# S5 output operators built by VectorE, and all of layer 1's S5 operators built in the buffer of layer 0's states

## The chip, the cores and the metric

The kernel runs on one core of a Trainium2 chip. Its engines are TensorE (PE in the profile; its weight loads are PEld), VectorE (DVE), ScalarE (ACT), GpSimd (POOL) and SyncE (SP), which here issues every DMA from one queue, in order. Each engine works through its own instructions in order and waits on semaphores for the others. The metric is the device time of one execution in microseconds; smaller is better.

## What is computed

The reference is a two-layer backbone over 256 context and 512 latent tokens of width 1024. Each layer normalizes and modulates the tokens, projects them once, sends parts of the result through three scans (Mamba-2 SSD, gated linear attention GLA, and S5), joins them, projects back and adds the residual. The S5 part is what the change touches. Its operators depend on parameters alone, not on the tokens:

```
lam_bar = jnp.exp(lam * jnp.exp(log_step[d].astype(f32))[:, None])
b_bar = ((lam_bar - 1.0) / lam)[..., None] * bmat
cmat = lax.complex(c_re[d].astype(f32), c_im[d].astype(f32))

def scan_fn(u, h0):
    bu = jnp.einsum("blgh,gph->blgp", u.astype(jnp.complex64), b_bar)
    h = s5_scan(bu, h0, lam_bar)
    return jnp.einsum("blgp,ghp->blgh", h, cmat).real, h[:, -1]
...
y_c, y_l = bidirectional(make_scan(0), make_scan(1), ctx_args, lat_args, h0)
```

There are 32 groups of 16 channels, each with 64 complex states, in two directions and two layers.

## The kernel before

The 768 tokens of a channel are cut into 96 blocks of 8 steps. For one layer the S5 part runs in these steps:

- `s5_lambda(l)` computes the powers 0 to 8 of `lam_bar` (tile `s5p`, 128 x 576; the eighth also in tile `l8`) by some 90 small DVE instructions on 128 x 32, transposes by PE, and a matrix for the input side that goes to DRAM (`lpD`).
- `s5_in_map(l, bi)`, eight times, loads a block of B (`in_s5b`) and a block of `lpD`, multiplies them on DVE (L360 to L363) and leaves an operator `bl` of 128 x 1024.
- the channels `u` come from four projection tiles and are regrouped through DRAM; PE multiplies them by `bl` (L608), and ACT, L612 and L613 fill the recurrence's input `st` (tile `xy`).
- the recurrence over 96 blocks is the loop at L643 to L646: four DVE instructions a step, 25 steps a layer, with scratch `hn` in buffer `bA`; then ACT and DVE copy the states into `hn`.
- `s5_out_map(l, bi)`, sixteen times, builds in a buffer `cs` the output operators: one POOL instruction on 128 x 32 (L375) and six on 128 x 288 (L380 to L385), two stores to `clD`, eight PE products (L394), two copies by ACT, two small DVE instructions (L400, L401) and two stores to `gD`.
- the output `y5` is three PE products a group (L687 to L689), from `gD`, `clD` and `hn`.

The other parts named below: the projections (PE L492 and L494, whose weights are loaded into `wr`, copied by ACT into `wh`, and whose rest `wl` is formed at L416 on POOL or, every third time, on DVE); the gates (L511); GLA (PE L732 for its gates, DVE L738 to L799); the convolution in front of SSD (DVE L856 to L865); the SSD scan, whose first instruction on DVE is the mask at L910.

In layer 0 the kernel before builds, ahead of its own projections, the operators of layer 1 too: `s5_lambda(1)` and the eight `s5_in_map(1)` work in one half of `bA`. What they make goes to DRAM: the powers to `pwD`, the input operators to `blD`. The sixteen `s5_out_map(1)` come after `y5`. Layer 1 loads the input operators two at a time, inside the loop that fills `st`.

Buffers carry a tag and a count: `bA` and `bB` have one each, `cs` three, `s5p` and `l8` one each, `wr` two. A tile that takes a tag waits until the earlier holder is done with it, in the order of the program. Within that a scheduler sets each engine's order from its own estimate of the times.

Of the kernel before, what the change touches and what calls it, by code (L numbers as in the profile page):

```python
# [41 lines left out]
def hybrid_backbone_kernel(  # L42
# [146 lines left out]
    pwD = dram([128, 704], "pwD1")  # L189
# [47 lines left out]
    pw0, l8_0 = T("s5p", [128, 576], 1), T("l8", [128, 128], 1)  # L237
# [126 lines left out]

    def s5_out_map(l, bi, pw, buf):

        gs = 2 * bi
        w5, tmp, cb, cn = cuts(buf, 576, 288, 128, 32)
        gt = tmp[:, 0:240]
        dma(cb, s5cb[l, bi])  # L370
        b0 = cb[:, 64:128].rearrange("p (a x) -> p a x", a=2)

        w54 = w5.rearrange("p (a g k h) -> p a g k h", a=2, g=2, k=9)
        t54 = tmp.rearrange("p (g k h) -> p g k h", g=2, k=9)
        G.tensor_scalar(cn, cb[:, 0:32], -1.0, None, MUL)  # L375
        shp = [128, 2, 9, 16]
        pr, pi = (pw[:, :, a, gs : gs + 2].rearrange("p k g -> p g k").unsqueeze(3).to_broadcast(shp) for a in range(2))
        cr, ci, cm = (x.rearrange("p (g h) -> p g h", g=2).unsqueeze(2).to_broadcast(shp)
                      for x in (cb[:, 0:32], cb[:, 32:64], cn))
        G.tensor_tensor(w54[:, 0], pr, cr, MUL)  # L380
        G.tensor_tensor(t54, pi, ci, MUL)
        G.tensor_tensor(w54[:, 0], w54[:, 0], t54, SUB)  # L382
        G.tensor_tensor(w54[:, 1], pi, cm, MUL)
        G.tensor_tensor(t54, pr, ci, MUL)
        G.tensor_tensor(w54[:, 1], w54[:, 1], t54, SUB)  # L385
        for d in range(2):
            h = slice(64 * d, 64 * d + 64)
# [88 lines left out]
    def layer(l, u):  # L476
# [117 lines left out]
        if not last:  # L594
            for bi in range(16):
                s5_out_map(0, bi, pw_(pw0), cs())
        st = T("xy", [128, 8, NT], 1).rearrange("p a t -> p (a t)").rearrange("p (i r g) -> p i r g", i=96, r=2)
        for bi in range(16):
            if bi % 2 == 0:
                blt = bls[bi // 2] if not last else wa[:, 4096 + 1024 * (bi // 2 % 2) : 5120 + 1024 * (bi // 2 % 2)]  # L600
                if last:
                    dma(blt, blD[bi // 2])
            bl = blt.rearrange("p (a g x) -> p a g x", a=2, g=4)[:, :, 2 * (bi % 2) : 2 * (bi % 2) + 2, :]
# [494 lines left out]
        for m in range(8):  # L1098
# [32 lines left out]
    s5_lambda(0, cs(), cs(), cs(512), cs(), cs(), pw0, l8_0)  # L1131
# [18 lines left out]
    t = [bct(), bct()]  # L1150
    wa0, wb0 = big("bA"), big("bB")
    bls = [wb0[:, 1024 * i : 1024 * i + 1024] for i in range(6)] + [wa0[:, 4096 + 1024 * i : 5120 + 1024 * i] for i in range(2)]
    lps, bbs = [a[:, 0:1024] for a in t], [a[:, 1024:1536] for a in t]
    for bi in range(8):
        s5_in_map(0, bi, lps[bi % 2], bbs[bi % 2], wa0[:, 3360:3872], bls[bi])
# [9 lines left out]
    u = norm_in(1, hx, nrm)  # L1165
    hx, acc = layer(1, u)
# [93 lines left out]
```

## Time and profile before

| | |
|---|---|
| median of three runs | 1703.96 us (1702.16 to 1710.37) |
| profiled execution | 1712.97 us, span 1711.3 us |
| PE busy | 1418.1 us (83%) |
| DVE busy | 1168.2 us (68%) |
| POOL busy | 783.2 us (46%) |
| ACT busy | 679.9 us (40%) |
| mean granted TensorE clock | 0.901 |

Busy shares are means over the whole span. The rows further down cut it into stretches, since another engine sets the pace in each. Layer 0 ends near 1050 us. The profiled execution is 9 us longer than the median of the runs.

### The profile page before, as it was taken

The page shows a single profiled execution, that of the slowest core. Times are in us where ns is not written, and L with a number is a line of the kernel's source. Part 1 is how long each engine was busy: PE and PEld are TensorE (multiplying, and loading weights), DVE is VectorE, ACT ScalarE, POOL GpSimd, SP SyncE. Part 2 cuts the span into 40 slices and gives each one's busy share as a digit, 9 for nine tenths or more (in the row PEclk, how much of TensorE's full clock was granted, in tenths as well). Part 3 has the DMA queues.
Part 4 walks back from the last instruction along what each step waited for, and adds up shares of the span by engine and source line. Part 5 has one row for each costly group of instructions (what it writes and reads, how often), then busy time and mean ns, then how long its engine had stood idle before and what let it go on. Part 6 is the DMA issues. An engine that isn't in the chain of part 4 may idle for free.

```text
span 1711.3 us, 23539 instructions
## 1 busy us (share of the span) xinstructions
PE 1418.1 (83%) x8536; PEld 1145.2 (67%) x8536; DVE 1168.2 (68%) x1992; ACT 679.9 (40%) x1220; POOL 783.2 (46%) x716
## 2 busy tenths in 40 slices
PE   3867766888989779977779999997889989967886
PEld 2656655777966557755668786886678777745665
DVE  7977558995477567679994127289835986688752
ACT  4312223225342336646553124343345345545442
POOL 3615647632268843445463141164123323656454
PEclk9788987898988889988889999998988999988998
DMA  8474654332543354444455745522363242344542
GB/s 308 124 185 135 178 150 135 93 118 71 176 123 86 100 165 140 142 154 139 128 187 188 282 135 178 189 85 80 111 193 107 64 139 93 119 138 145 184 131 96
DMA packets 139885, 243.55 MB, mean 142 GB/s; under 512 B 31992, under 2 KB 72568, under 8 KB 139768
## 3 DMA queue, kind: packets, MB, share of 16 engines
q1 hardware_dynamic: 139768, 242.04, 45.3%
q8 instruction: 67, 1.10, 0.3%
q14 instruction: 50, 0.41, 0.1%
HBM read 192.81 MB, written 49.18 MB: 141 GB/s over the span
## 4 chain that ended last, share of the span: by engine, by line
PE 25%; DVE 18%; DMA 13%; POOL 6%; issue 4%; ACT 4%; SPq 0%; DVEq 0%; ACTq 0%; POOLq 0%
PE pl L492 7%; PE pl L1062 6%; DMA bA<-acsD 5%; DMA bB<-acsD 3%; PE pc L494 2%; PE pc L1064 2%; DVE xy L863 1%; DMA wr<-in_wblk 1%; ACT bA L121 1%; POOL wl L416 1%; DVE bB L916 1%; DVE bA L916 1%; DVE xy L645 1%; DMA cs<-zD 1%; DVE bA L644 1%
## 5 line engine op out<-in xcount | busy, mean ns | idle before, releaser
L492 PE MATMUL pl<-hl,wh 128*128 128x512 f32 (+1 forms) x1184 | 411.5, 414 | 15.9 <-DVE ev L511 12.3
L416 POOL TENSOR_TENSOR wl<-wr,wh 128x1024 fp32r<-128x1024 f32 (+1 forms) x82 | 210.4, 2566 | 308.5 <-ACT wh L121 284.6
L492 PEld LDWEIGHTS pl<-hl,wh 128*128 128x128 f32 (+1 forms) x1184 | 226.0, 195 | 73.5 <-DVE ev L511 13.6
L492 PE MATMUL pl<-hl,wl 128*128 128x512 f32 (+1 forms) x592 | 243.5, 412 | 20.0 <-POOL wl L416 10.7
L121 ACT ACTIVATE wh<-wr 128x1024 fp32r<-128x1024 f32 (+1 forms) x122 | 127.6, 1047 | 283.7 <-PE pc L1064 69.3
L494 PE MATMUL pc<-hl,wh 128*128 128x256 f32 (+1 forms) x864 | 202.0, 304 | 11.3 <-DVE ev L511 7.2
L494 PEld LDWEIGHTS pc<-hl,wh 128*128 128x128 f32 (+1 forms) x864 | 152.5, 202 | 26.1 <-DVE ev L511 8.7
L492 PEld LDWEIGHTS pl<-hl,wl 128*128 128x128 f32 (+1 forms) x592 | 115.4, 195 | 49.1 <-POOL wl L416 12.0
L494 PE MATMUL pc<-hl,wl 128*128 128x256 f32 (+1 forms) x432 | 128.6, 298 | 0.0
L1062 PE MATMUL pl<-hl,wh 128*128 128x512 f32 x256 | 87.7, 419 | 16.9 <-ACT hl L121 4.6
L394 PE MATMUL pa<-cs 64*32 64x128 f32 x512 | 42.9, 305 | 64.0 <-POOL cs L382 27.3
L494 PEld LDWEIGHTS pc<-hl,wl 128*128 128x128 f32 (+1 forms) x432 | 87.3, 202 | 2.7 <-issue 1.7
L121 ACT ACTIVATE ev<-pl 128x512 f32<-128x512 f32 (+1 forms) x96 | 51.1, 534 | 87.7 <-PE pl L709 43.9
L709 PE MATMUL pl<-wh,hl 128*128 128x256 f32 x384 | 79.6, 307 | 2.6 <-ACT ev L121 2.6
L416 DVE TENSOR_TENSOR wl<-wr,wh 128x1024 fp32r<-128x1024 f32 x40 | 55.4, 1386 | 38.3 <-ACT wh L121 38.1
L121 ACT ACTIVATE bB<-bB 128x512 f32<-128x512 f32 (+4 forms) x40 | 45.7, 1142 | 85.1 <-DMA bB<-acsD 52.3
L394 PEld LDWEIGHTS pa<-cs 64*32 64x32 f32 x512 | 21.5, 115 | 80.6 <-POOL cs L382 28.9
L863 DVE SCALAR_TENSOR_TENSOR xy<-ev,par_sb,xy 128x512 f32<-128x512 f32 (+1 forms) x112 | 74.8, 704 | 0.6
L375 POOL TENSOR_SCALAR cs<-cs 128x32 f32<-128x32 f32 x32 | 20.1, 629 | 118.4 <-DMA cs<-in_s5cb 43.3
L709 PEld LDWEIGHTS pl<-wh,hl 128*128 128x128 f32 x384 | 66.9, 214 | 7.8 <-ACT ev L121 3.8
L1062 PEld LDWEIGHTS pl<-hl,wh 128*128 128x128 f32 x256 | 49.8, 199 | 31.1 <-ACT hl L121 6.7
L709 PE MATMUL pl<-wl,hl 128*128 128x256 f32 x192 | 58.4, 308 | 3.8 <-DVE wl L416 3.8
(483 smaller groups left out, 3604.4 us busy)
## 6 DMA issues: line engine op xcount, KB each, us to landing
wr<-in_wblk SPq DMA_DIRECT2D x80, 512.0 KB
wr<-in_wout SPq DMA_DIRECT2D x32, 512.0 KB
hl<-in_mod_w SPq DMA_DIRECT2D x20, 512.0 KB
bA<-acsD SPq DMA_DIRECT2D x10, 1024.0 KB
bB<-acsD SPq DMA_DIRECT2D x10, 1024.0 KB
clD<-cs SPq DMA_DIRECT2D x64, 128.0 KB
cs<-clD SPq DMA_DIRECT2D x32, 256.0 KB
cs<-in_mod_w SPq DMA_DIRECT2D x16, 512.0 KB
```

The source lines that it names most:

```text
L121: return S.activation(out, in_, f, **kw)
L375: G.tensor_scalar(cn, cb[:, 0:32], -1.0, None, MUL)
L394: PE.matmul(pk[d][32 * gg : 32 * gg + 32], b0[64 * d : 64 * d + 64, a, :], w54[64 * d : 64 * d + 64, a, gg, d : 8 + d, :].rearrange("p k h ...
L416: (eng or (V if wcount[0] % 3 == 0 else G)).tensor_tensor(wl, wr, wh.bitcast(F32), SUB)
L492: PE.matmul(p_l[:m], lhs, u[k][:, ui, LC:NT], start=st, stop=sp)
L494: PE.matmul(p_c[:m], lhs, u[k][:, ui, 0:LC], start=st, stop=sp)
L644: V.tensor_tensor(tr[:, 1, :n], li, src[:, :, ::-1], MUL)
L709: PE.matmul(p, u[k][:, ui, 128 * c : 128 * c + 128], ws[k // 4][wi][:, 256 * (k % 4) : 256 * (k % 4) + 256], start=n == 0, stop=n == 23)
L863: V.scalar_tensor_tensor(ac, raw[:, o + k : o + k + n], pcol("cw", w0 + k), ac, MUL, ADD)
L916: V.scalar_tensor_tensor(rf[:, h, :], rbw[:, h, :], rb[:, ih : ih + 1], rf[:, h, :], SUB, MIN)
L1062: PE.matmul(p_l, lhs, rhs[kk][:, ui, LC - t0 : NT - t0], start=st, stop=sp)
L1064: PE.matmul(p_c, lhs, rhs[kk][:, ui, 0:LC], start=st, stop=sp)
```

## The change

Three things change.

- `s5_out_map` gives its work on 128 x 288 to DVE. The negated copy `cn` (one instruction on 128 x 32) is gone; the sign is put in by the last of now six DVE instructions.
- `s5_lambda(1)` and the `s5_in_map(1)` move from the head of layer 0 behind its `y5`, into a new holder of `bA`, and take turns with the sixteen `s5_out_map(1)`. The powers of layer 1 stay in `s5p` and `l8`; `pwD` is gone.
- Layer 1 loads its eight input operators from `blD` at once, six into `bB` and two into `bA`, ahead of its projections.

```
@@ -362,27 +361,40 @@
             blo = bl[:, 512 * o : 512 * o + 512]
             V.tensor_tensor(blo, blo, tb, SUB if o == 0 else ADD)
 
+    def s5_in_maps(l):
+        if l == 1:
+            wa, wb = big("bA"), big("bB")
+            out = [wb[:, 1024 * i : 1024 * i + 1024] for i in range(6)] + [wa[:, 1024 * i : 1024 * i + 1024] for i in range(2)]
+            for bi in range(8):
+                dma(out[bi], blD[bi])
+            return out
+        t = [bct(), bct()]
+        wa, wb = big("bA"), big("bB")
+        out = [wb[:, 1024 * i : 1024 * i + 1024] for i in range(6)] + [wa[:, 1024 * i : 1024 * i + 1024] for i in range(2)]
+        for bi in range(8):
+            s5_in_map(l, bi, t[bi % 2][:, 0:1024], t[bi % 2][:, 1024:1536], wa[:, 2048:2560], out[bi])
+        return out
+
     def s5_out_map(l, bi, pw, buf):
 
         gs = 2 * bi
-        w5, tmp, cb, cn = cuts(buf, 576, 288, 128, 32)
+        w5, tmp, cb = cuts(buf, 576, 288, 128)
         gt = tmp[:, 0:240]
         dma(cb, s5cb[l, bi])
         b0 = cb[:, 64:128].rearrange("p (a x) -> p a x", a=2)
 
         w54 = w5.rearrange("p (a g k h) -> p a g k h", a=2, g=2, k=9)
         t54 = tmp.rearrange("p (g k h) -> p g k h", g=2, k=9)
-        G.tensor_scalar(cn, cb[:, 0:32], -1.0, None, MUL)
         shp = [128, 2, 9, 16]
         pr, pi = (pw[:, :, a, gs : gs + 2].rearrange("p k g -> p g k").unsqueeze(3).to_broadcast(shp) for a in range(2))
-        cr, ci, cm = (x.rearrange("p (g h) -> p g h", g=2).unsqueeze(2).to_broadcast(shp)
-                      for x in (cb[:, 0:32], cb[:, 32:64], cn))
-        G.tensor_tensor(w54[:, 0], pr, cr, MUL)
-        G.tensor_tensor(t54, pi, ci, MUL)
-        G.tensor_tensor(w54[:, 0], w54[:, 0], t54, SUB)
-        G.tensor_tensor(w54[:, 1], pi, cm, MUL)
-        G.tensor_tensor(t54, pr, ci, MUL)
-        G.tensor_tensor(w54[:, 1], w54[:, 1], t54, SUB)
+        cr, ci = (x.rearrange("p (g h) -> p g h", g=2).unsqueeze(2).to_broadcast(shp)
+                  for x in (cb[:, 0:32], cb[:, 32:64]))
+        V.tensor_tensor(w54[:, 0], pr, cr, MUL)
+        V.tensor_tensor(t54, pi, ci, MUL)
+        V.tensor_tensor(w54[:, 0], w54[:, 0], t54, SUB)
+        V.tensor_tensor(w54[:, 1], pi, cr, MUL)
+        V.tensor_tensor(t54, pr, ci, MUL)
+        V.scalar_tensor_tensor(w5[:, 288:576], w5[:, 288:576], -1.0, tmp, MUL, SUB)
         for d in range(2):
             h = slice(64 * d, 64 * d + 64)
             dma(clD[l][bi][h].rearrange("p (g x) -> p g x", g=4),
@@ -568,16 +580,6 @@
             dma(acsD[l][:, d].rearrange("c h l -> h c l"), rows.rearrange("h (c l) -> h c l", c=6))
 
 
-        wa = wa0 if not last else big("bA")
-        if not last:
-            sv, wk, lt, tw, tu, pwl = cuts(wa, 480, 512, 512, 576, 576, 704)
-            s5_lambda(1, sv, wk, lt, tw, tu, pwl[:, 0:576], pwl[:, 576:704])
-            dma(pwD, pwl)
-            for bi in range(8):
-                lp = wa[:, 1024 * (bi % 2) : 1024 * (bi % 2) + 1024]
-                bb, tb, bl = cuts(wa[:, 2048:4096], 512, 512, 1024)
-                s5_in_map(1, bi, lp, bb, tb, bl)
-                dma(blD[bi], bl)
         for i in range(4):
             p_c, p_l = proj(BU + i, early=last and i == 0)
             e_ = ev()
@@ -593,14 +595,10 @@
         ug = lambda g: ugs[g // 16][:, g % 16]
         if not last:
             for bi in range(16):
-                s5_out_map(0, bi, pw_(pw0), cs())
+                s5_out_map(0, bi, pw_(s5p[0][0]), cs())
         st = T("xy", [128, 8, NT], 1).rearrange("p a t -> p (a t)").rearrange("p (i r g) -> p i r g", i=96, r=2)
         for bi in range(16):
-            if bi % 2 == 0:
-                blt = bls[bi // 2] if not last else wa[:, 4096 + 1024 * (bi // 2 % 2) : 5120 + 1024 * (bi // 2 % 2)]
-                if last:
-                    dma(blt, blD[bi // 2])
-            bl = blt.rearrange("p (a g x) -> p a g x", a=2, g=4)[:, :, 2 * (bi % 2) : 2 * (bi % 2) + 2, :]
+            bl = bls[bi // 2].rearrange("p (a g x) -> p a g x", a=2, g=4)[:, :, 2 * (bi % 2) : 2 * (bi % 2) + 2, :]
             pst = (px, ps)[bi % 2](384)
             for gg in range(2):
                 for a in range(2):
@@ -611,10 +609,7 @@
             act(st[0:64, :, :, gsl], pv[0:64], AF.Copy)
             V.tensor_copy(st[64:128, 0:32, :, gsl], pv[64:128, 31::-1])
             V.tensor_copy(st[64:128, 32:96, :, gsl], pv[64:128, 95:31:-1])
-        l8t = l8_0
-        if last:
-            l8t = T("l8", [128, 128], 1)
-            dma(l8t, pwD[:, 576:704])
+        l8t = s5p[l][1]
 
         pt8 = cs().rearrange("p (k a r) -> p k a r", k=8, a=2)
         V.tensor_copy(pt8[:, 0], l8t.rearrange("p (a r) -> p a r", a=2))
@@ -664,9 +659,6 @@
             act(hn[lo_, rr, 32:96], st[lo_, 31:95, rr], AF.Copy)
             act(hn[hi_, rr, 32:96], st[hi_, 94:30:-1, rr], AF.Copy)
         hn = hn.rearrange("p r c g -> p r g c")
-        if not last:
-            pw1 = T("s5p", [128, 576], 1)
-            dma(pw1, pwD[:, 0:576])
         c0 = 32 if last else 0
         ncx = 96 - c0
 
@@ -692,8 +684,18 @@
                 dma(y5D[l][b4 // 2].rearrange("t (h g) c -> (t h) g c", h=16), y5[:, 4 * b4 - 4 : 4 * b4 + 4, :])
 
         if not last:
+
+            s5p.append((T("s5p", [128, 576], 1), T("l8", [128, 128], 1)))
+            wa = big("bA")
+            s5_lambda(1, *cuts(wa, 480, 512, 512, 576, 576), *s5p[1])
             for bi in range(16):
-                s5_out_map(1, bi, pw_(pw1), cs())
+                s5_out_map(1, bi, pw_(s5p[1][0]), cs())
+                if bi % 2:
+                    b = bi // 2
+                    lp, bl = (wa[:, 1024 * j + 1024 * (b % 2) :][:, 0:1024] for j in (0, 2))
+                    bb, tb = cuts(wa[:, 4096 + 1024 * (b % 2) :], 512, 512)
+                    s5_in_map(1, b, lp, bb, tb, bl)
+                    dma(blD[b], bl)
         for i in range(4):
             spill(BQ + i, qkD[l][128 * i : 128 * i + 128], t0 if i < 2 else 0)
 
```

The rest of the diff creates the list `s5p`, calls `s5_in_maps` for both layers and drops the tile `l8` from one small ACT instruction.

SP's queue in layer 0, ahead of the recurrence, before: the loads and stores of `s5_in_map(1)` (`bA`, `blD`) stand between those of `s5_out_map(0)` (`cs`, `clD`, `gD`).

```order
L354 DMA bA_484<-lpD_131 128x1x1024 x2
L388 DMA clD_134<-cs_1210 256x1x128 x2
L370 DMA cs_1264<-in_s5cb 128x128
L388 DMA clD_134<-cs_1237 256x1x128 x2
L403 DMA gD_136<-cs_1210 16x240
L404 DMA gD_136<-cs_1210 16x240
L353 DMA bA_484<-in_s5b 128x1x512
L354 DMA bA_484<-lpD_131 128x1x1024
L580 DMA blD_133<-bA_484 128x1024
L370 DMA cs_1291<-in_s5cb 128x128
```

SP's queue behind the last stores of `y5`, in the changed kernel:

```order
L339 DMA lpD_131<-bA_1776 128x4x128
L424 DMA wr_4605<-in_wblk 128x1024
L353 DMA bA_1776<-lpD_131 128x1x1024 x2
L424 DMA wr_4682<-in_wblk 128x1024
L400 DMA clD_134<-cs_1893 256x1x128 x2
L400 DMA clD_134<-cs_1919 256x1x128 x2
L400 DMA clD_134<-cs_1954 256x1x128 x2
L352 DMA bA_1776<-in_s5b 128x1x512
L353 DMA bA_1776<-lpD_131 128x1x1024
L352 DMA bA_1776<-in_s5b 128x1x512
L353 DMA bA_1776<-lpD_131 128x1x1024
```

The rows on layer 1's operators have moved from ahead of the recurrence to behind `y5`; loads of projection weights (`wr`) stand between them.

DVE before, at the first mask of the SSD scan (L910): the convolution and gates stand in front of it.

```order
L865 SCALAR_TENSOR_TENSOR xy_4123<-ev_5074,xy_4123 128x256
L865 SCALAR_TENSOR_TENSOR xy_4123<-ev_5074,xy_4123 128x512
L511 SCALAR_TENSOR_TENSOR ev_6119<-ev_6119,pl_6070 128x512
L416 TENSOR_TENSOR wl_6189<-wr_6186,wh_6188 128x1024
L511 SCALAR_TENSOR_TENSOR ev_6119<-ev_6119,pc_66 128x256
L210 TENSOR_TENSOR modp<-pa_3597,par_sb 128x16
L910 TENSOR_TENSOR bA_5138<-pa_5141,LE 128x128
L911 TENSOR_TENSOR bA_5138<-pa_5141,GE 128x128
L918 SCALAR_TENSOR_TENSOR bA_5138<-bA_5138,dts_616 128x128 x7
```

DVE in the changed kernel, behind the last instruction of `s5_lambda(1)` (the numbers of lines have grown: L392 to L397 are the new instructions of `s5_out_map`, L736 was L738, L858 to L867 were L856 to L865):

```order
L392 TENSOR_TENSOR cs_1893<-s5p_1774,cs_1893 128x288
L392 TENSOR_TENSOR cs_1919<-s5p_1774,cs_1919 128x288
L392 TENSOR_TENSOR cs_1954<-s5p_1774,cs_1954 128x288
L393 TENSOR_TENSOR cs_1893<-s5p_1774,cs_1893 128x288
L395 TENSOR_TENSOR cs_1893<-s5p_1774,cs_1893 128x288
L393 TENSOR_TENSOR cs_1919<-s5p_1774,cs_1919 128x288
L395 TENSOR_TENSOR cs_1919<-s5p_1774,cs_1919 128x288
L393 TENSOR_TENSOR cs_1954<-s5p_1774,cs_1954 128x288
L395 TENSOR_TENSOR cs_1954<-s5p_1774,cs_1954 128x288
L865 SCALAR_TENSOR_TENSOR xy_4090<-ev_4314,par_sb,xy_4090 128x512
L736 TENSOR_SCALAR m_268_2961<-ps_2967,par_sb 128x256
L865 SCALAR_TENSOR_TENSOR xy_4090<-ev_4314,par_sb,xy_4090 128x256
```

Layer 1's output operators, GLA and the convolution now share DVE's queue there. Counted over the whole order, 493 DVE instructions stand between the first of `s5_lambda(1)` and the first mask: 121 of the convolution, 105 of GLA, about 100 each of `s5_lambda(1)` and of the new form, 48 of the input operators; 28 of GLA, 13 of the convolution and 9 of the gated norm come behind the mask and stood ahead of it before.

PE before, at the first product of GLA's gates (L732):

```order
L394 MATMUL pa_1357<-cs_1345 32x128 x2
L709 MATMUL pl_2663<-wh_2652,hl_457 128x256
L709 MATMUL pl_2663<-wl_2653,hl_457 128x256
L732 MATMUL ps_3000<-bB_2995 128x256
L732 MATMUL ps_3004<-bB_2995 128x512
L732 MATMUL ps_3008<-bB_2995 128x256
L709 MATMUL pl_2663<-wh_2658,hl_462 128x256 x2
```

PE in the changed kernel, at the transposes of `s5_lambda(1)` (L337) and GLA's gates (L734):

```order
L504 MATMUL pl_4341<-hl_441,wl_4338 128x512
L504 MATMUL pl_4341<-hl_446,wh_4337 128x512 x2
L504 MATMUL pl_4341<-hl_446,wl_4338 128x512
L504 MATMUL pl_4341<-hl_451,wh_4337 128x512
L337 MATMUL ps_1880<-ident,bA_1776 128x128 x4
L734 MATMUL ps_2967<-bB_2962 128x256
L734 MATMUL ps_2971<-bB_2962 128x512
L504 MATMUL pl_4341<-hl_451,wh_4337 128x512
L504 MATMUL pl_4341<-hl_451,wl_4338 128x512
```

GLA's gates stood among the value projections (L709), with the output operators of layer 0 in front (L394). They now stand behind the transposes of `s5_lambda(1)` and four projection tiles of the convolution, as their PSUM tiles (`ps`) come behind those of the transposes.

## Rows read from the trace of the kernel before

**Rows 1.** Which engine was busy how long in each stretch of the span (busy us, instructions).
```profile
0.00:60.00 60.00, 29.96 (x266) 19.16 (x267) 49.20 (x167) 26.55 (x44) 20.02 (x25) 0.89 0.76 258
60.00:290.00 230.00, 167.54 (x1065) 138.04 (x1063) 158.99 (x299) 54.06 (x107) 121.15 (x122) 0.83 0.55 153
290.00:408.00 118.00, 103.87 (x655) 88.19 (x654) 109.31 (x180) 28.75 (x47) 61.27 (x65) 0.94 0.35 106
408.00:470.00 62.00, 53.47 (x387) 49.19 (x386) 20.54 (x42) 36.17 (x31) 13.54 (x20) 0.83 0.45 134
470.00:658.00 188.00, 152.93 (x1048) 116.91 (x1048) 125.80 (x213) 62.84 (x129) 129.24 (x164) 0.88 0.45 130
658.00:905.00 247.00, 200.66 (x1135) 159.58 (x1134) 210.22 (x326) 143.00 (x318) 127.05 (x81) 0.90 0.44 144
905.00:1087.00 182.00, 177.61 (x1112) 140.71 (x1111) 61.35 (x96) 53.03 (x78) 45.48 (x23) 0.98 0.53 185
1087.00:1275.00 188.00, 164.55 (x1027) 142.39 (x1025) 140.63 (x220) 76.77 (x94) 68.88 (x60) 0.92 0.41 129
```

**Rows 2.** Costliest POOL lines of `s5_out_map`: count, busy us, mean ns, idle before and its cause.
```profile
L380 POOL TENSOR_TENSOR cs<-s5p,cs 128x288 f32<-128x288 f32 x32 | 34.7, 1084 | 0.0
L384 POOL TENSOR_TENSOR cs<-s5p,cs 128x288 f32<-128x288 f32 x32 | 27.3, 857 | 0.9
L375 POOL TENSOR_SCALAR cs<-cs 128x32 f32<-128x32 f32 x32 | 20.1, 629 | 118.4 <-DMA cs<-in_s5cb 43.3 <-DVE bA L361 18.8 <-DMA clD<-cs 16.1
```

**Rows 3.** POOL lines between 470 and 658 us, while layer 1's output operators are built.
```profile
L416 POOL TENSOR_TENSOR wl<-wr,wh 128x1024 fp32r<-128x1024 f32 x7 | 17.8, 2547 | 0.0
L375 POOL TENSOR_SCALAR cs<-cs 128x32 f32<-128x32 f32 x15 | 10.3, 688 | 21.3 <-DMA cs<-in_s5cb 18.9 <-PE pa L394 1.2 <-ACT ev L121 0.8
```

**Rows 4.** Waits of PE between 60 and 290 us: total us, times, longest.
```profile
PE pa L394 <- POOL cs L382: 27.0, 6, 9.4
PE pa L394 <- DVE cs L400: 12.9, 6, 5.3
```

**Rows 5.** Waits of DVE between 60 and 290 us: total us, times, longest.
```profile
DVE bA L360 <- DMA blD<-bA: 15.6, 4, 7.0
DVE bA L361 <- DMA bA<-in_s5b: 15.5, 5, 4.5
```

**Rows 6.** DVE lines, whole kernel: shapes, count, busy us, mean ns, idle before.
```profile
L348 DVE TENSOR_TENSOR s5p<-cs,cs 64x288 f32<-64x288 f32 x2 | 0.9, 450 | 0.0
L348 DVE TENSOR_TENSOR bA<-bA 64x288 f32<-64x288 f32 x2 | 1.8, 904 | 0.0
L360 DVE TENSOR_TENSOR bA<-bA 128x512 f32<-128x512 f32 x16 | 12.1, 789 | 23.7 <-DMA blD<-bA 15.6 <-DMA bA<-lpD 8.1
L361 DVE TENSOR_TENSOR bA<-bA 128x512 f32<-128x512 f32 x16 | 18.2, 1135 | 25.8 <-DMA bA<-in_s5b 15.5 <-issue 10.2
L251 DVE SCALAR_TENSOR_TENSOR bA<-bA 128x32 f32<-128x32 f32 x12 | 4.3, 358 | 0.0
L284 DVE SCALAR_TENSOR_TENSOR bA<-bA 128x32 f32<-128x32 f32 x6 | 1.1, 180 | 0.0
```

**Rows 7.** DVE lines between 266 and 408 us: the S5 recurrence and GLA.
```profile
L645 DVE TENSOR_TENSOR xy<-xy,bA 128x64 f32<-128x64 f32 (+2 forms) x25 | 22.2, 888 | 0.0
L755 DVE TENSOR_TENSOR_SCAN m<-sm,m 64x768 f32<-64x768 uint8 x4 | 8.5, 2123 | 0.1
L789 DVE SCALAR_TENSOR_TENSOR bB<-bB,dcs,ps 64x128 f32<-64x128 f32 x22 | 7.8, 354 | 0.7
L787 DVE SCALAR_TENSOR_TENSOR bB<-bB,dcs,ps 64x128 f32<-64x128 f32 x22 | 7.4, 338 | 0.5
L754 DVE TENSOR_TENSOR_SCAN m<-sm,m 64x768 f32<-64x768 uint8 x4 | 7.3, 1834 | 0.0
```

**Rows 8.** One line's instructions: shortest, median, longest ns, first and last start.
```profile
L910 DVE TENSOR_TENSOR bA<-pa,LE x10: 271/275/291, 658.0 to 1555.7; 128x128 f32<-128x128 f32 x10
```

**Rows 9.** Waits of DVE between 1087 and 1275 us, layer 1's S5 stretch.
```profile
DVE xy L612 <- ACT xy L121: 31.8, 14, 16.4
```

More of the change, by code (lines that the diff above doesn't have):

```diff
@@ L188, in hybrid_backbone_kernel @@
     lpD = [dram([512, 128], f"lpD{l}") for l in range(2)]
-    pwD = dram([128, 704], "pwD1")
     blD = dram([8, 128, 1024], "blD1")
@@ L234, in mod_tiles @@
         mod_cols(l, b0, nb, rows)
-    pw0, l8_0 = T("s5p", [128, 576], 1), T("l8", [128, 128], 1)
+    s5p = [(T("s5p", [128, 576], 1), T("l8", [128, 128], 1))]
     pw_ = lambda t: t.rearrange("p (k a g) -> p k a g", k=9, a=2)
@@ L1112, in layer @@
             if m == 6:
-                act(ho[:, 0:1] if last else T("l8", [128, 128], 1)[:, 0:1], acc[:, 0:1], AF.Ln, scale=0.0, bias=1.0)
+                act(ho[:, 0:1], acc[:, 0:1], AF.Ln, scale=0.0, bias=1.0)
         return hx2, (acc, sq)
@@ L1130, in hybrid_backbone_kernel @@
     rsqrt_rows(buf[0])
-    s5_lambda(0, cs(), cs(), cs(512), cs(), cs(), pw0, l8_0)
+    s5_lambda(0, cs(), cs(), cs(512), cs(), cs(), *s5p[0])
     tA, tB = big("bA"), big("bB")
@@ L1149, in hybrid_backbone_kernel @@
     u = norm_in(0, hx, nrm)
[L1150 to L1155, printed above, removed]
+    bls = s5_in_maps(0)
     hx, acc = layer(0, u)
@@ L1165, in hybrid_backbone_kernel @@
     u = norm_in(1, hx, nrm)
+    bls = s5_in_maps(1)
     hx, acc = layer(1, u)
```

## Prediction

> **What bounds the kernel now.** I read the busy times by stretch first [rows 1]. From 905 to 1087 us TensorE (PE) is busy 177.6 of 182 us and sets the pace almost alone, and the change touches nothing there. What can be won or lost lies elsewhere: the S5 part of layer 0 (60 to 470 us), the building of layer 1's output operators beside the convolution (470 to 658) and, smaller, layer 1's S5 stretch (1087 to 1275). The reader is to see that nothing is saturated in the first of these: between 60 and 290 us PE is busy 167.5 of 230 us and VectorE (DVE) 159.0. From 290 to 408 the S5 recurrence has DVE busy 109.3 of 118: that stretch is DVE's. Then 408 to 470 holds the copies of the states and the y5 products, with DVE at 20.5 of 62. From 470 to 658 GpSimd (POOL) is busy 129.2 of 188 and DVE 125.8; the first mask of the SSD scan starts at 658.0 [rows 8]. From 658 to 905 DVE is busy 210.2 of 247 and PE 200.7; both are near their limit.
>
> The chain of waits before 290 us goes through what is changed. PE waits 27.0 us for L382 and 12.9 for L400, both in `s5_out_map` [rows 4]. DVE waits in `s5_in_map` of layer 1: 15.6 us for the stores of `blD`, 15.5 for the loads of `in_s5b` [rows 5]; the recurrence can't start before these, as its scratch buffer is the same `bA`. POOL in turn idles 118.4 us ahead of L375, for its loads, for DVE and for its own stores [rows 2].
>
> **The change, part by part.**
>
> 1. S5 output operators on DVE. POOL loses 32 x 7 instructions: six lines between 27.3 and 34.7 us and one of 20.1 [rows 2], about 200 us. DVE gets 32 x 6 = 192 instructions on 128 x 288. Its nearest row is 0.450 us for 64 x 288 with quiet neighbours, and 0.904 for the same form beside a busy POOL [rows 6]. These are my two bounds: 86 to 174 us, 43 to 87 per layer. I take 0.45, since the POOL work that made the neighbours slow is largely what goes.
>
> 2. Layer 0 up to the recurrence. DVE's 159.0 us between 60 and 290 lose `s5_in_map(1)` (12.1 + 18.2 = 30), `s5_lambda(1)` (about 90 small instructions, 0.18 to 0.36 us each by L284 and L251, so 16 to 32; I take 20 as POOL grows quieter) and the GLA scans L755 and L754 (16) [rows 6, 7], and gain 43. That makes 136 us. With the waits for `blD` and `in_s5b` gone I put DVE at 85% instead of 69%: 160 us, so the recurrence starts at about 220 instead of 290. It keeps its 109 us less the GLA lines L787 and L789 (15), 94 us: it ends at about 314. PE can follow that only if its waits of 40 us [rows 4] shrink, because the last gates stand between the recurrence's steps. State copies and y5 take the 62 us they take now [rows 1]. So `s5_lambda(1)` starts at about 380 (360 to 400).
>
> 3. From `s5_lambda(1)` to the SSD scan. This is the price of the move: what was spread over idle time is now one piece of DVE's queue. Today DVE has 20.5 + 125.8 = 146 us between 408 and 658 [rows 1]. The order puts some 50 of those instructions (28 of GLA, 13 of the convolution, 9 of the gated norm) behind the first mask; at 0.34 us as L787 to 0.89 as L645 [rows 7] that is 17 to 44, I take 26. To the rest come the GLA lines that today run beside the recurrence (8.5 + 7.8 + 7.4 + 7.3 = 31 [rows 7]), because their PSUM buffers now come behind those of `s5_lambda(1)`, then lambda (20), the input maps (30) and the output maps (43). Sum: 146 - 26 + 31 + 20 + 30 + 43 = 244 us. Today's durations were taken beside a POOL busy for 129 us, which falls to about 30 without `s5_out_map` [rows 1, 3]; I take 236. Nothing hides them: PE had only 152.9 us of work between 470 and 658. How well DVE is fed decides. Its queue is in order, and mixes work that waits for PE (convolution, GLA), for ACT and for SP's stores and loads; between 470 and 658 it reached 67%, in the recurrence 93% [rows 1]. I take 89%: 265 us, so the first mask at 645, 13 us ahead of today. The bounds: at 95% with 225 us and a start at 360 it is 597; at 80% with 260 us and a start at 400 it is 725. On SP's queue the store of `lpD` and the stores of `clD` now stand ahead of weight loads `wr`; a load that is late there stops PE, then the convolution, then DVE.
>
> 4. The SSD stretch. 26 us of DVE work go into a stretch where DVE has 37 us of idle time and PE 46 [rows 1]. At least part lengthens it: 0 to 26 us, I take 16.
>
> 5. Layer 1. All eight blocks of `blD` are loaded ahead, so the waits of 31.8 us in filling the recurrence's input [rows 9] shrink. That ACT waits for a matmul on a block that has not landed is not in that row, only that DVE waits for ACT. PE idles 23.4 us in this stretch [rows 1], which is all that can come back; 4 MB of loads ahead of the weights can also cost. 0 to 23, I take 8.
>
> Sum: -13 + 16 - 8 = -5 us against the profiled 1713.0, and so 1699 against the median of the runs, 1704.0, 9 us below it. The round trip of `pwD` (one store, two loads) goes too, and so does `s5_out_map`'s negation; both lay beside longer waits, so I count them as nothing. If that cover were missing they would be worth 1 or 2 us.
>
> **One rule weighed.** Beside a busy POOL the 64 x 288 form took 0.904 us against 0.450 [rows 6], and POOL's own L380 had a mean of 1.084 us. The Trainium skill, SBUF — State Buffer, section "Who interferes with whom", says that a VectorE instruction with two inputs in SBUF contends with a GpSimd instruction that reads SBUF. The new DVE instructions are all of that kind. The trace agrees for the row named; whether it is this contention in each instance no row shows. By the rule the price of the 192 depends on how much of POOL's reading they still meet; that is rival C.
>
> **Rivals.**
>
> A. DVE is not fed in part 3 and SSD starts later: slower. For it: all of DVE's work there is in one in-order queue with a store and a load behind almost every operator, today's share there is 67%, and PE, which had only 35 us of idle time between 470 and 658, would idle for about half of a longer stretch. Against it: out of the 188 us today much is POOL's pace (21.3 us idle ahead of L375 alone [rows 3]), which goes. At 80%, 244 us take 305, SSD starts at 685, 27 us late; with 26 in the SSD stretch and nothing in layer 1 it is +53, so 1757; halfway to the forecast 1728. It decides when the share falls below about 85%, with SSD at 658 or later.
>
> B. A larger gain. The waits in front of 290 us vanish altogether, lambda starts at 365, DVE runs at 95% on 230 us: SSD at 607, -51 us; +10 and -12 behind it give -53, so 1651; halfway 1675. For it: the recurrence's 93%; against it: PE must then deliver its gates 70 us earlier too, and has run at 73% there.
>
> C. POOL still costs DVE. L416 remains on POOL (7 of 2.55 us in 188 us [rows 3]). If every new instruction cost 0.904 us, 43 us more would stand in part 2 (51 at 85%) and 43 in part 3 (48 at 89%), and the total would be 1798; halfway between the bounds, at 0.68 us, 1748. Against it: POOL's remaining share between 470 and 658 is 33 of 188 us, 18%, and if only those instructions that meet it paid the double, it would be 16 us.
>
> D. The gain and the loss cancel because PE sets the pace all the way: within 0.5%. That is the edge of the forecast itself.
>
> **How the numbers follow.** Forecast, 1699, own range 1685 to 1714: chance 0.32. A, 1714 to 1757: 0.35. B, 1650 to 1685: 0.26. C: 0.07, 1715 to 1798. No change, as far as a measurement of this kernel tells, is within 0.5%, 8.5 us: 1695 to 1712. Faster is B and 0.13 of the forecast, 0.39; the same 0.17 of the forecast and 0.03 of A, 0.20; slower the rest, 0.41. The range from 1650 to 1750 leaves out the far end of A and of B, about 2 in 10.
>
> **What would show it.** First instruction of the recurrence at about 220 (against 290); first of `s5_lambda(1)` at 360 to 400; first mask of SSD at about 645; 192 DVE instructions on 128 x 288 at a mean near 0.45 us; DVE's share between lambda and SSD near 89%; the SSD stretch 10 to 20 us longer than 247. The prediction fails if PE does not reach the gates earlier (then the recurrence ends where it ends now and everything behind is added), or if DVE's share in part 3 lies at 80% or at 95%.

## The result, and the profile after

The changed kernel takes 1765.11 us (median of 4 runs, 1762.41 to 1772.7), the kernel before 1703.06 us on the same chip. The ratio is 1.0363 (95% interval 1.0318 to 1.0408): 3.6% slower. The profiled execution has a span of 1771.0 us, against 1711.3. The page's busy row:

```profile
PE 1430.6 (81%) x8536; PEld 1158.0 (65%) x8536; DVE 1171.4 (66%) x2184; ACT 674.5 (38%) x1214; POOL 610.9 (34%) x492
```

POOL has lost 172 us of busy time (783.2 before) and DVE has gained 3 (1168.2 before), though the six new lines are busy 91 us. So older DVE instructions have got shorter. In part this belongs to this kernel alone: where the output operators change engine and nothing moves (e1_out_dve below), DVE's busy time grows by 25 us, to 1193.3. These are two of DVE's six lines on 128 x 288, and the form that had 904 ns in [rows 6]:

```profile
L392 DVE TENSOR_TENSOR cs<-s5p,cs 128x288 f32<-128x288 f32 x32 | 17.4, 548 | 25.6 <-DMA cs<-in_s5cb 23.7 <-DMA clD<-cs 1.2 <-issue 0.7
L394 DVE TENSOR_TENSOR cs<-cs 128x288 f32<-128x288 f32 x32 | 13.9, 449 | 0.1
L347 DVE TENSOR_TENSOR s5p<-bA 64x288 f32<-64x288 f32 x2 | 0.9, 450 | 0.0
```

So the price was right: 0.45 us, with two of the six lines, L392 and L393, near 0.55. The reason given for it holds for the one form that can be compared: the 64 x 288 form on `bA` ran beside POOL's `s5_out_map` before, at 904 ns, and is at 450 ns now. This agrees with what the Trainium skill says in SBUF — State Buffer, "Who interferes with whom", that VectorE with two inputs in SBUF contends with GpSimd's reads. Busy time is not what the change costs. The view of stretches, cut where the steps of the changed kernel begin and end (PE, PEld, DVE, ACT, POOL busy us, then the granted clock), shows where the time went:

```profile
60.00:208.00 148.00, 122.62 (x846) 98.71 (x845) 97.14 (x222) 34.76 (x83) 20.10 (x9) 0.91 0.55 144
208.00:296.00 88.00, 71.71 (x473) 64.70 (x472) 73.69 (x120) 16.46 (x29) 39.08 (x31) 0.94 0.27 87
296.00:369.00 73.00, 54.88 (x353) 50.80 (x352) 6.30 (x10) 32.68 (x25) 5.35 (x8) 0.84 0.49 151
369.00:635.00 266.00, 184.68 (x1211) 142.41 (x1210) 237.78 (x523) 76.70 (x146) 71.70 (x90) 0.80 0.42 122
635.00:728.00 93.00, 86.55 (x542) 74.14 (x541) 42.84 (x77) 31.18 (x49) 31.02 (x18) 0.93 0.31 100
728.00:941.00 213.00, 166.01 (x938) 130.56 (x937) 160.06 (x289) 118.07 (x282) 97.27 (x65) 0.86 0.48 153
941.00:1064.00 123.00, 113.96 (x706) 90.05 (x705) 47.65 (x61) 42.87 (x49) 52.56 (x24) 0.96 0.58 204
1064.00:1366.00 302.00, 266.56 (x1569) 227.06 (x1568) 181.32 (x304) 114.57 (x163) 89.22 (x77) 0.87 0.42 133
```

The marks behind these cuts, from the lines' instructions (first and last start, layer 0 first):

```profile
L638 DVE TENSOR_TENSOR bA<-cs,xy x50: 207/686/2226, 208.6 to 1251.1; 128x64 f32<-128x64 f32 x22, 128x768 f32<-128x768 f32 x14, 128x704 f32<-128x704 f32 x7, 128x512 f32<-128x512 f32 x7
L260 DVE COPY bA<-bA x1: 184/184/184, 369.4 to 369.4; 128x32 f32<-128x32 f32 x1
L734 PE MATMUL ps<-bB x32: 374/532/692, 397.0 to 1184.6; 32*128 32x256 f32 x16, 32*128 32x512 f32 x16
L912 DVE TENSOR_TENSOR bA<-pa,LE x10: 277/282/294, 635.1 to 1615.0; 128x128 f32<-128x128 f32 x10
L912 DVE TENSOR_TENSOR bB<-pa,LE x10: 276/280/294, 728.3 to 1630.4; 128x128 f32<-128x128 f32 x10
L835 POOL TENSOR_TENSOR m<-m,bB x2: 4926/5847/6768, 721.5 to 1434.3; 128x3072 f32<-128x3072 f32 x1, 128x2048 f32<-128x2048 f32 x1
```

The same marks of the kernel before, as far as [rows 8] does not have them: the mask of the second group, GLA's last instruction, the last line of SSD's decay factors (up to 1000 us), and the last statistic of layer 0:

```profile
L910 DVE TENSOR_TENSOR bB<-pa,LE x10: 271/277/292, 664.0 to 1570.4; 128x128 f32<-128x128 f32 x10
L833 POOL TENSOR_TENSOR m<-m,bB x2: 4796/5792/6787, 590.0 to 1384.6; 128x3072 f32<-128x3072 f32 x1, 128x2048 f32<-128x2048 f32 x1
L916 DVE SCALAR_TENSOR_TENSOR bB<-bB,dts x48: 332/339/2486, 610.9 to 858.4; 128x128 f32<-128x128 f32 x48
L1161 PE MATMUL ps<-ev,ones x4: 379/538/592, 1023.8 to 1024.8; 128*128 128x256 f32 x2, 128*128 128x512 f32 x2
```

Read them against [rows 1] and [rows 8]. The recurrence starts at 208.6 us instead of 290.8 and y5 is done at 364, 106 us earlier than before. `s5_lambda(1)` starts at 369. The first SSD mask follows at 635.1, 23 us earlier than before. Up to here the change is a gain. But that is the mask of group 0, in `bA`. The mask of group 1, in `bB`, comes at 728.3, while before it stood 6 us behind that of group 0, at 664. `bB` is held by GLA, whose last instruction, L835 on POOL, starts at 721.5 and takes 6.8 us; it stood at 590.0 before. Between 635 and 728 DVE is busy 42.8 of 93 us. The SSD scan, taken up to the last of those decay instructions, ends at 941 instead of 860. PE has used those 93 us (86.6 busy) for projections that came later before, and gives 41 us back behind the scan: layer 0's last statistic on PE starts at 1063.0 instead of 1023.8.

```profile
L1158 PE MATMUL ps<-ev,ones x4: 379/538/592, 1063.0 to 1064.0; 128*128 128x256 f32 x2, 128*128 128x512 f32 x2
```

So layer 0 is 39 us longer, and layer 1 another 20 (1771.0 - 1063 against 1711.3 - 1024).

### The profile page after: what moved, and what is told of

Same layout as the page of the kernel before. It is cut to its first block, busy times and chain, and to the rows that moved or that the text cites. A ratio compares the mean times of both kernels' runs of the same rounds, so it can differ in the third digit from the quotient of the medians.

```text
span 1771.0 us, 23423 instructions
## 1 busy us (share of the span) xinstructions
PE 1430.6 (81%) x8536; PEld 1158.0 (65%) x8536; DVE 1171.4 (66%) x2184; ACT 674.5 (38%) x1214; POOL 610.9 (34%) x492
## 5 line engine op out<-in xcount | busy, mean ns | idle before, releaser
L504 PE MATMUL pl<-hl,wh 128*128 128x512 f32 (+1 forms) x1184 | 404.2, 408 | 14.1 <-ACT ev L121 9.4
L504 PEld LDWEIGHTS pl<-hl,wh 128*128 128x128 f32 (+1 forms) x1184 | 224.0, 193 | 70.1 <-ACT ev L121 10.3
L504 PE MATMUL pl<-hl,wl 128*128 128x512 f32 (+1 forms) x592 | 242.0, 409 | 11.4 <-POOL wl L428 9.8
L506 PEld LDWEIGHTS pc<-hl,wh 128*128 128x128 f32 (+1 forms) x864 | 156.1, 208 | 28.5 <-ACT ev L121 11.6
L504 PEld LDWEIGHTS pl<-hl,wl 128*128 128x128 f32 (+1 forms) x592 | 113.9, 192 | 41.2 <-POOL wl L428 11.9
L1064 PE MATMUL pl<-hl,wh 128*128 128x512 f32 x256 | 95.1, 441 | 12.5 <-ACT bA L121 4.0
L406 PE MATMUL pa<-cs 64*32 64x128 f32 x512 | 44.6, 313 | 53.8 <-issue 29.9
L865 DVE SCALAR_TENSOR_TENSOR xy<-ev,par_sb,xy 128x512 f32<-128x512 f32 (+1 forms) x112 | 75.0, 703 | 0.3
L406 PEld LDWEIGHTS pa<-cs 64*32 64x32 f32 x512 | 23.2, 118 | 71.0 <-issue 35.8
L523 DVE SCALAR_TENSOR_TENSOR ev<-ev,pl 128x512 f32<-128x512 f32 x32 | 21.9, 684 | 63.7 <-ACT ev L121 63.5
```

Of the source, the lines that this page charges most:

```text
L406: PE.matmul(pk[d][32 * gg : 32 * gg + 32], b0[64 * d : 64 * d + 64, a, :], w54[64 * d : 64 * d + 64, a, gg, d : 8 + d, :].rearrange("p k h ...
L504: PE.matmul(p_l[:m], lhs, u[k][:, ui, LC:NT], start=st, stop=sp)
L506: PE.matmul(p_c[:m], lhs, u[k][:, ui, 0:LC], start=st, stop=sp)
L523: V.scalar_tensor_tensor(e_[:, a:b], e_[:, a:b], 1.0, p, ADD, MUL)
L865: V.scalar_tensor_tensor(ac, raw[:, o + k : o + k + n], pcol("cw", w0 + k), ac, MUL, ADD)
L1064: PE.matmul(p_l, lhs, rhs[kk][:, ui, LC - t0 : NT - t0], start=st, stop=sp)
```

## The experiments

Four explanations were put to the test. Theory 1: GLA stands behind layer 1's lambda, because its PSUM tiles take the same ring (`ps`, three buffers) later in the program, and holds `bB`. Theory 2: VectorE's load in one piece in front of the SSD scan. Theory 3: layer 1's loads ahead. The fourth, that the price of the new instructions is at fault, falls with the rows above. All ratios are to runs of the kernel before on the same chip.

**Output operators on VectorE alone** (e1_out_dve). The kernel before, with the new `s5_out_map` for both layers:

```
-        G.tensor_tensor(w54[:, 0], pr, cr, MUL)
+        V.tensor_tensor(w54[:, 0], pr, cr, MUL)
...
```

> The kernel before, with only the S5 output operators given to VectorE; nothing is moved. Theory 1 (the loss comes from GLA standing behind the operators of layer 1, not from VectorE's new work): the 192 new instructions cost 0.45 us each, waits of TensorE for them shrink, total 1690 to 1712 us. Theory 2 (VectorE's load as such is what costs): 86 us more on VectorE, of which a third to a half shows, total 1730 to 1745 us.

Measured: 1709.64 us, ratio 1.0027 (1.0005 to 1.0049). This half of the change is close to neutral. Its stretches, cut at the start of the recurrence (278) and at its end (402):

```profile
60.00:278.00 218.00, 180.09 (x1168) 145.79 (x1167) 158.15 (x389) 56.85 (x113) 22.44 (x13) 0.89 0.62 172
278.00:402.00 124.00, 87.85 (x519) 74.15 (x518) 112.92 (x175) 25.24 (x40) 58.19 (x52) 0.86 0.27 80
```

The recurrence starts 13 us earlier, with PE busy 83% ahead of it instead of 73%, but it takes 124 us and ends at 402 as before; DVE is busy 112.9 of the 124, and its busy time over the kernel is 25 us longer (1193.3). The six new lines have means of 0.45 to 0.67 us there. Theory 2 in the form "86 us more on VectorE must show" is out.

**The move alone** (e2_move_pool). The changed kernel with `s5_out_map` of the kernel before, on GpSimd:

```
-        V.tensor_tensor(w54[:, 0], pr, cr, MUL)
+        G.tensor_tensor(w54[:, 0], pr, cr, MUL)
...
```

> The changed kernel, with the output operators given back to GpSimd; the move stays. Theory 1: GLA is as late as in the change, and GpSimd builds sixteen operators in the piece in front of SSD, total 1755 to 1790 us. Theory 2: VectorE loses 86 us, 43 of them in front of the first SSD mask, total 1720 to 1745 us.

Measured: 1775.32 us, ratio 1.0445 (1.0399 to 1.049). So the loss lies in the move and the loads ahead, which this kernel keeps; beside them VectorE's operators are a gain of some 10 us (1765 against 1775). The two first masks stand as far apart as in the change:

```profile
L913 DVE TENSOR_TENSOR bA<-pa,LE x10: 270/276/293, 649.7 to 1617.1; 128x128 f32<-128x128 f32 x10
L913 DVE TENSOR_TENSOR bB<-pa,LE x10: 271/276/299, 738.0 to 1632.5; 128x128 f32<-128x128 f32 x10
```

**Layer 1 loads two at a time again** (e3_lazy_load), the rest as changed:

```
-    bls = s5_in_maps(1)
+    bls = None
...
+            if last:
+                if bi % 2 == 0:
+                    dma(blt, blD[bi // 2])
```

> The changed kernel, with layer 1 loading its input operators two at a time inside the filling loop, as before. Theory 1: TensorE was saturated while the input was filled, so loading ahead gained and lost nothing, total 1760 to 1772 us. Theory 3 (the eight loads ahead cost layer 1 the 19 us that it is longer): 1742 to 1750 us.

Measured: 1746.97 us, ratio 1.0254 (1.0229 to 1.0279). Here Theory 1 missed and Theory 3 holds: 18 us of the loss come from the loads ahead. The stretch from layer 1's start to its convolution takes 280 us in this kernel, with this row:

```profile
1060.00:1340.00 280.00, 250.50 (x1566) 211.50 (x1565) 181.68 (x293) 114.97 (x159) 84.88 (x74) 0.92 0.45 141
```

In the changed kernel the same stretch, 1064 to 1366, takes 302 us, with nearly the same count of PE instructions (1569 against 1566), 266.6 us of PE busy time instead of 250.5, and a granted clock of 0.87 instead of 0.92. PE's work is no larger, it runs slower. Cut finer, at the y5 products, the changed kernel shows how long the clock stays at its lower level (0.50 of 2.4 GHz is 1.2 GHz):

```profile
1258.00:1264.00 6.00, 4.20 (x34) 3.45 (x34) 3.31 (x10) 5.96 (x3) 1.82 (x4) 1.00 0.20 61
1264.00:1270.00 6.00, 2.42 (x9) 1.46 (x8) 0.00 (x0) 5.99 (x2) 0.00 (x1) 0.54 0.01 5
1270.00:1276.00 6.00, 4.82 (x23) 4.82 (x23) 1.38 (x2) 4.31 (x6) 3.66 (x2) 0.50 0.20 55
1276.00:1282.00 6.00, 6.00 (x30) 6.00 (x29) 0.00 (x0) 1.46 (x2) 1.01 (x1) 0.50 0.66 187
1282.00:1288.00 6.00, 6.00 (x30) 6.00 (x30) 0.00 (x0) 0.98 (x2) 0.00 (x0) 0.50 0.45 110
```

and the kernel with the loads two at a time, at the same place:

```profile
1274.00:1280.00 6.00, 2.59 (x24) 2.35 (x22) 0.00 (x0) 5.99 (x2) 0.00 (x0) 0.94 0.38 109
1280.00:1286.00 6.00, 4.87 (x23) 4.88 (x24) 2.58 (x3) 5.07 (x8) 3.71 (x2) 0.50 0.18 53
1286.00:1292.00 6.00, 6.00 (x30) 4.73 (x30) 4.11 (x7) 5.33 (x7) 4.31 (x5) 0.70 0.68 188
1292.00:1298.00 6.00, 6.00 (x71) 5.70 (x70) 2.93 (x8) 1.58 (x3) 1.11 (x1) 1.00 0.70 196
```

In both PE has just waited for the copies of the states, and the clock falls. In the first it stays at half from 1264 to 1288 and some 6 us beyond, with PE busy in every microsecond of the last two rows; in the second it is back within 12 us. In both, the rise follows the return of the projection products (L504), of which the first behind the wait starts at 1291.0 in the changed kernel and at 1287.4 in the other; until then PE runs products of y5 and GLA. Why the clock comes back sooner in one of them, no run tests.

**One word for GLA's place** (e5_lambda_pa), the rest as changed:

```
-        pt = ps()
+        pt = (ps, pa)[l]()
```

> The changed kernel, with one word changed: the four transposes of layer 1's lambda take their PSUM tile from the ring of two (pa) in place of the ring of three (ps) that GLA uses. Theory 1: GLA's gates start near 220 us in place of 397, GLA is done near 560, both groups of SSD have their first mask near 620 to 650, total 1680 to 1715 us. Theory 2: the same work stands in front of the masks on VectorE's queue, total 1745 to 1772 us.

Measured: 1745.08 us, ratio 1.0243 (1.0219 to 1.0267), 20 us of the loss. The marks:

```profile
L734 PE MATMUL ps<-bB x32: 374/532/692, 198.5 to 1164.3; 32*128 32x256 f32 x16, 32*128 32x512 f32 x16
L912 DVE TENSOR_TENSOR bA<-pa,LE x10: 273/276/292, 666.1 to 1592.9; 128x128 f32<-128x128 f32 x10
L912 DVE TENSOR_TENSOR bB<-pa,LE x10: 271/274/293, 673.4 to 1608.3; 128x128 f32<-128x128 f32 x10
```

The mechanism of Theory 1 is shown: GLA's gates start at 198.5 instead of 397, and the masks of the two groups stand 7 us apart. The size is not: the first mask comes at 666 and not near 620 to 650, and the total is outside Theory 1's range, at the lower edge of Theory 2's. GLA's instructions are now between those of the recurrence, which ends at 332 instead of 295, and y5 and lambda come later by as much. What undoing GLA's lateness gives is 20 us; layer 0 now ends at 1041.7, and the remaining 18 us against the kernel before (1023.8) have another cause.

**Both undone** (e6_pa_lazy):

> The changed kernel with both undone: lambda's transposes in the ring of two, and layer 1 loading two at a time. If the two losses are independent (GLA's place costs layer 0 about 20 us, the loads ahead cost layer 1 about 18), their gains add up: 1720 to 1732 us. If both act through the same stretch, the second gives little: 1738 to 1747 us.

Measured: 1722.7 us, ratio 1.0112 (1.0078 to 1.0146). The gains add up, as expected of two independent losses. What is left is layer 0, and this is its stretch from the end of y5 to the first mask:

```profile
403.00:666.00 263.00, 192.69 (x1262) 149.53 (x1263) 212.73 (x494) 70.21 (x140) 50.84 (x73) 0.84 0.49 144
```

It takes 263 us where 188 stood before [rows 1], for 68 us gained at the end of y5. DVE is busy 212.7 of it. The net loss is 8 us at the first mask (666 against 658) and 16 at the end of layer 0 (1039.8 against 1023.8).

**The loads ahead, alone** (e9_before_preload). The kernel before, with only layer 1's eight loads moved ahead:

```
-                blt = bls[bi // 2] if not last else wa[:, 4096 + ...]
-                if last:
-                    dma(blt, blD[bi // 2])
+                blt = bls[bi // 2]
```

> The kernel before with one part of the change alone: layer 1 loads its eight input operators ahead, into both buffers. If the loads ahead cost layer 1 by themselves: 1718 to 1725 us. If they cost only together with the other parts: 1698 to 1708 us.

Measured: 1728.51 us, ratio 1.0141 (1.0111 to 1.0171), a little above the first expectation. It costs 1.4% by itself, in a kernel that is not disturbed otherwise. From layer 1's start to its convolution, 1024 to 1323, it takes 299 us, against 285 before, 1024 to 1309. The rows of both, the kernel before first:

```profile
1024.00:1309.00 285.00, 256.66 (x1568) 217.26 (x1568) 182.11 (x293) 115.37 (x160) 85.40 (x76) 0.90 0.44 139
1024.00:1323.00 299.00, 262.80 (x1566) 222.78 (x1565) 181.30 (x304) 114.83 (x163) 89.33 (x77) 0.89 0.42 133
```

Of the 14 us, 6 are PE's busy time at the lower mean clock, and 8 its idle time. Where they come from shows in two pieces, the filling of the recurrence's input and the piece from the last product of y5 to the convolution. The kernel before:

```profile
1085.00:1119.00 34.00, 34.00 (x228) 30.92 (x227) 11.27 (x33) 13.14 (x24) 5.66 (x7) 1.00 0.57 186
1299.00:1309.00 10.00, 10.00 (x72) 8.38 (x72) 5.98 (x13) 3.33 (x8) 2.57 (x2) 1.00 0.44 143
```

and with the loads ahead:

```profile
1083.00:1102.00 19.00, 19.00 (x151) 18.15 (x150) 10.03 (x33) 9.55 (x19) 5.37 (x9) 1.00 0.28 78
1283.00:1323.00 40.00, 33.44 (x187) 28.53 (x183) 14.53 (x32) 14.45 (x26) 11.73 (x18) 0.87 0.42 123
```

The filling takes 15 us less, but PE idles in neither filling: 77 fewer of its instructions run there, projection products that ran between the products of the blocks before. They come back behind y5, where PE now needs 40 us instead of 10, waits in between and has a granted clock of 0.87 instead of 1.00. The changed kernel has the same two pieces (19 and 38 us).

**Layer 1's output operators on GpSimd, both undone** (e7_pool1). As e6_pa_lazy, with

```
+        E5 = (V, G)[l]
...
+        E5.tensor_tensor(w54[:, 0], pr, cr, MUL)
```

> As the run with both undone, and the output operators of layer 1 alone back on GpSimd, those of layer 0 stay on VectorE. If what is left of the loss in layer 0 is VectorE's load in front of the SSD scan, 43 us less of it show: 1695 to 1712 us. If GpSimd's pace takes its place, as in the run with all of them on GpSimd: 1725 to 1740 us.

Measured: 1715.74 us, ratio 1.0074 (1.0047 to 1.0101), between the two expectations. The first mask stays at 670: DVE's load falls by some 12 us in that stretch (201 us of 266), PE now waits for POOL's L395 and L406 instead. Less load, but a slower partner; it does not decide. The total is 7 us below e6_pa_lazy's, with intervals that overlap, and what is gained lies behind the mask.

**All of layer 1's operators later still** (e8_late). The block stands behind the SSD norm, beside the output projection, loads two at a time:

```
         yss = ssd_norm(0) + ssd_norm(1)
+        if not last:
+            s5_lambda(1, ...)
+            for b in range(8): s5_in_map(1, b, ...)
+            for bi in range(16): s5_out_map(1, bi, ...)
```

> The changed kernel with layer 1 loading two at a time, and all of layer 1's operators built later still, behind the SSD norm, beside the output projection, where VectorE is busy 69 of 163 us in the kernel before. Nothing then stands in front of the SSD scan but the convolution and GLA. If VectorE's load there is what costs, the first mask comes near 560 to 600 us and the total is 1665 to 1695 us. If TensorE is the bound from there on and pays the products of the operators in its own busy stretch: 1700 to 1725 us.

Measured: 1738.91 us, ratio 1.0209 (1.0178 to 1.0241). The total is above both expectations. The front does more than was expected, and the back takes more than that:

```profile
L907 DVE TENSOR_TENSOR bA<-pa,LE x10: 273/276/291, 541.9 to 1584.4; 128x128 f32<-128x128 f32 x10
771.00:1057.00 286.00, 211.24 (x1285) 162.17 (x1288) 183.39 (x363) 65.00 (x100) 73.22 (x33) 0.82 0.59 184
```

The first mask is at 541.9, 124 us ahead of e6_pa_lazy, so the operators are indeed what makes that stretch long. But the stretch behind the scan, 771 to 1057, takes 286 us, where the same projection took 164 before. PE is busy 211 of it at a clock of 0.82: the products of the operators, the modulation's products and the projection share PE's one queue, and 23 us of PE's waits there are for DVE's lines of the operators (L394, L397, L412).

**Only the input operators late** (e10_in_late). As e6_pa_lazy, with `s5_in_map(1)` behind the SSD norm; it has no PE work:

> As the run with both losses undone, and the eight input operators of layer 1 built late, beside the output projection; lambda and the output operators stay behind y5. The input operators take 30 to 38 us of VectorE in front of the SSD scan and need no product of TensorE, so if VectorE's load there is what is left, the first mask comes 25 to 40 us earlier than 666 us, the output projection grows by less than 15 us, and the total is 1685 to 1705 us. If the output projection pays what the front gains, as in the run with all operators late: 1715 to 1730 us.

Measured, in 12 runs: 1699.47 us, ratio 0.9972 (0.9952 to 0.9992), 0.3% faster than the kernel before, so the loss is gone and little more.

```profile
L914 DVE TENSOR_TENSOR bA<-pa,LE x10: 274/278/292, 626.7 to 1542.0; 128x128 f32<-128x128 f32 x10
403.00:627.00 224.00, 192.69 (x1254) 151.79 (x1255) 185.69 (x450) 73.53 (x144) 54.82 (x76) 0.87 0.40 122
```

The first mask is at 626.7, 40 us ahead of e6_pa_lazy, for 33 to 37 us of DVE work taken out of that stretch (48 instructions on 128 x 512 at 0.68 to 0.78 us, the means of L359 and L360 in the changed kernel). Between the rows of e6_pa_lazy and this one DVE's busy time falls by 27 us (212.7 to 185.7) and its idle time by 12 (50.3 to 38.3). The projection behind the scan pays 14 of it (178 us from the last decay instruction to the end of layer 0, against 164), and layer 0 ends 24 us earlier. This bears out Theory 2 in a narrower form: not the load on VectorE over the kernel counts, but what the move put into the one stretch in front of the scan. The input operators took their loads with them too. In e6_pa_lazy DVE waited in that stretch 14.6 us for `lpD` and, mostly once, for a block of `in_s5cb`:

```profile
DVE cs L392 <- DMA cs<-in_s5cb: 18.6, 2, 17.7
```

Here these waits are 0 and 3.4 us. How much of the 40 us is DVE's work and how much its loads, no run separates.

**The same with output operators on GpSimd** (e11_in_late_pool1):

> The same, with the output operators of layer 1 on GpSimd. If VectorE's load is all that is left in front of the SSD scan: 43 us less of it, first mask near 610 us, total 1675 to 1700 us. If GpSimd's pace for sixteen operators sets the stretch, the first mask stays near 660 to 670 us and the total is 1710 to 1725 us.

Measured, in 12 runs: 1707.78 us, ratio 1.0026 (1.0007 to 1.0046). First mask at 639, so later than with VectorE building them, and between the two expectations. In this arrangement VectorE is the better place for layer 1's output operators, by 0.5%; between e7_pool1 and e6_pa_lazy it was the other way round, by 0.4%, with intervals that overlap. So the runs don't settle the place in general.

## Why the prediction failed

The time, 1765, lies outside the range of 1650 to 1750, and the forecast's sign was wrong: 5 us faster was forecast, 62 us slower was measured.

- Part 1, the price of the new instructions: right. 0.45 to 0.55 us against 0.45.
- Part 2: right in kind, a little too cautious. Recurrence at 209 (220), its end at 295 (314), lambda at 369 (380).
- Part 3: right in the sum and in the share: DVE 237.8 us (236) in 266 us (265), 89%; the first mask at 635 (645). That it is right to 2 us is in part luck. By the lines of that stretch `s5_lambda(1)` took 26 us (20), the input operators 33 (30), and GLA's lines 62, more than the 29 of before and the 31 added. The convolution made up for it, at 80 us where it had 97 before.
- Part 4 is the step that failed: "26 us of DVE work go into a stretch where DVE has 37 us of idle time ... I take 16". I had counted the GLA instructions behind the first mask as load for DVE, and had not asked which buffer they hold. They hold `bB`, which SSD's second group needs. From the first mask to the end of the scan it took 306 us instead of 202, 104 more where 16 were forecast. 87 of them are the second group's: its mask came 93 us behind the first and not 6. 41 came back in the output projection. Undoing GLA's place gave 20 us and not all 39 (e5_lambda_pa), since GLA's work then stands in the recurrence's way. For the other 18, e10_in_late and e8_late point to the moved operators in front of the scan: with the input operators behind it the loss is gone. Whether they cost by DVE's work or by their loads stays open.
- Part 5 had the wrong sign: -8 was forecast, and it is +18 by e3_lazy_load, +22 by e6_pa_lazy against e5_lambda_pa, and +24 by e9_before_preload (1.4%). The filling did get shorter: DVE's wait for ACT is 22.8 us now, and 31.8 in [rows 9]; in either, some 16 us are one wait.

```profile
DVE xy L610 <- ACT xy L121: 22.8, 13, 16.2
```

  But a stretch in which PE is saturated gives nothing back when it gets shorter; the same PE instructions were still to be done. The part took PE's idle time in that stretch, 23 us, as what could come back, and asked only whether the loads would delay the weights. It did not ask where the projection products go that ran beside the loads: they went behind y5, into waits and a lower clock. The kernel with the loads two at a time and the changed one differ there by 16 us of PE's busy time and by 6 of its idle time; e9_before_preload and the kernel before by 6 and 8. What brings the clock down, and how much of the loss it makes, is not shown.
- The rivals: A named the right sign, but for another place. Its test, the first mask at 658 or later, came out against it, and the kernel was slower all the same. B's mark for the first mask (607) was missed and C is out (0.45 to 0.55 us), and so is D: the loss is 3.6%, not within 0.5%. None of them named a buffer that is held by a scan which has become late.

In sum, by the profiled spans: -23 up to the first mask, +104 in the SSD scan, -41 in the output projection, +20 in layer 1: +60, as measured (1771.0 - 1711.3). By the experiments, the ratio falls from 1.0363 to 1.0243 with GLA back in its place, to 1.0112 with the loads two at a time too, and to 0.9972 with the input operators behind the scan.

## What to carry to other kernels

Where a move puts work behind an allocation from a shared ring of buffers, look which other work takes its tiles from that ring later in the program, what buffer that work holds to its end, and who waits for the buffer: the delay shows there, not at the moved work. A first mark that comes earlier proves nothing when the stage has two halves with a buffer each; predict the mark of the last one too. An early load in front of an engine that is saturated buys nothing, so ask where the work goes that ran beside the loads.

## What the runs showed that was not expected

- The same 1566 to 1569 PE instructions took 250.5 or 266.6 us of busy time, by granted clocks of 0.92 or 0.87; after a wait of some 7 us around 1264 us the clock stood at 0.50 for over 24 us though PE was busy in all of the last 12 of them.
- Giving POOL's 128 x 288 instructions to DVE made DVE's busy time grow by 25 us (1168.2 to 1193.3, e1_out_dve), and in the changed kernel by 3 (1171.4), for 91 us of new work in the latter. The form that went from 904 to 450 ns is one example of an older instruction that is shorter without POOL's work beside it; how much of the rest has that cause is not shown.
